# Room of 32 bytes between the parts of the activation in the feed-forward phase of a two-layer encoder

## The chip, the cores and the metric

The kernel runs on one core of a Trainium2 chip. The core has a matrix engine (PE, with its weight loads listed as PEld), a vector engine (DVE), a scalar engine (ACT), GpSimd (POOL), and a queue engine (SP) that only starts transfers here. All of them work on a memory of 128 partitions (SBUF); PE writes its sums to PSUM. The metric is the device time of one execution in microseconds (us), as the median of three runs: 2537.42 us before the change (2535.24 to 2538.15).

## The reference

The kernel computes two layers of an encoder on 512 tokens of width 1024, in float32. Each layer has a feed-forward block, a mixer of three kinds of attention, and a second feed-forward block; each sits between two RMS norms:

```python
def swiglu(x, w_gu, w_down):
    gate, up = jnp.split(x @ w_gu, 2, axis=-1)
    return (jax.nn.silu(gate) * up) @ w_down

for l in range(DEPTH):                        # DEPTH = 2, D_FF = 2816
    y = swiglu(rmsnorm(h, ffn1_pre_g[l]), ffn1_w_gu[l], ffn1_w_down[l])
    h = h + 0.5 * rmsnorm(y, ffn1_post_g[l])
    u = rmsnorm(h, mix_pre_g[l])
    ...                                       # projections, three attentions, gates
    h = h + rmsnorm(merged @ w_out[l], mix_post_g[l])
    y = swiglu(rmsnorm(h, ffn2_pre_g[l]), ffn2_w_gu[l], ffn2_w_down[l])
    h = h + 0.5 * rmsnorm(y, ffn2_post_g[l])
```

The change touches the four feed-forward blocks only.

## The kernel before

Everything is kept transposed: a tile has 128 features on the partitions and the 512 tokens along the row, which is 2048 bytes per partition. A float32 product is made of three products of the short float32 form (fp32r): each operand is split into `hi` (the value rounded) and `lo` (the rest), and `mm3` (lines 235, 236, 237) adds hi·hi, hi·lo and lo·hi in one PSUM bank. ACT writes `hi`, DVE writes `lo` by subtraction: for weights at lines 193 and 194 (tiles `wh`, `wl`, made from the raw block `wr`), for activations at lines 258 and 259 in `split`. Weights stream in by transfers that ACT's queue starts (line 179).

A feed-forward block (`ffn`) first makes 22 gate columns and 22 up columns from the normed input `X` (8 pairs `hi`, `lo`); `finish` (lines 425 to 427) scales the gate sum with `rB`, applies Silu, multiplies with the up sum and splits the result into a pair of the tag `a`. These 22 pairs, 44 tiles, are the activation's parts. Then the down projection (`end`) reads them as the moving operand: 8 output columns of 22 blocks each, the last column in two halves of the tokens, so that the norm of the first half can run beside the second. The first three columns of the next block (`begin`) also run in two halves, and two of their weight tiles are held in slots of the phase's own pool (`w`, tag `a` in a feed-forward block, `tx` in the mixer).

Memory: one pool (`sb`) lasts for the whole kernel, with X, h, the weights and the temporaries. Behind it each phase opens a pool of its own at the same place (`open_phase`), first a feed-forward pool, then a mixer pool, then a feed-forward pool, for each layer. A tile of a new phase has to wait for the last reader or writer of those tiles of the old phase that lay on the same bytes. At the start of the mixer, SP fetches from DRAM the tables `mask` (line 554) and `tab` (550) and the bias block `braw` (560), and stores h (`kept`, 544); DVE uses the masks at line 567, POOL uses `tab` at line 551.

Each engine works through its own list of instructions in order. The lists are made by a scheduler at build time, which also looks at which slots of a pool are free.

Of the kernel before, what the change touches and what calls it, by code (L numbers as in the profile page):

```python
# [10 lines left out]
F32 = mybir.dt.float32  # L11
# [5 lines left out]
P = 128  # L17
# [6 lines left out]
KF = FF // P  # L24
# [86 lines left out]
def encoder_kernel(ctx: ExitStack, tc: tile.TileContext, order, xT, wts, cols, rows, rpb, consts, tables, out):  # L111
# [12 lines left out]

    def open_phase(kind):
        pool = ExitStack()
        phase[0] = (kind, pool.enter_context(tc.tile_pool(name=nm("ph"), bufs=1, reuse_waits="tile")))
        phase[0][1].tile([P, PAD[kind]], F32, tag="pad", name=nm("pad"), bufs=1)
        return pool
    serial = [0]  # L130

    def nm(s):
        serial[0] += 1
        return f"{s}{serial[0]}"

    def big(tag, dt=F32, shape=(P, T), name="v"):
        if tag in BUFS:
            return sb.tile(list(shape), dt, tag=tag, name=nm(name), bufs=BUFS[tag])
        kind, pool = phase[0]
        return pool.tile(list(shape), dt, tag=tag, name=nm(name), bufs=ABUFS[kind][tag])  # L140

    def small(tag, w=4, bufs=4):
# [39 lines left out]
    def ensure(n):  # L182
        while stream["made"] < min(n, NTILES * 2):
            i = stream["made"]
            if i // 2 == len(stream["raw"]):
                fetch(1)
            raw = stream["raw"][i // 2][:, i % 2 * HB : i % 2 * HB + HB, :]
            if i in stream["held"]:
                tag = stream["held"][i]
                hi, lo = (big(tag, F32R, (P, HB, P), name="w") for _ in range(2))  # L190
            else:
                hi, lo = (sb.tile([P, HB, P], F32R, tag=t, name=nm(t), bufs=BUFS[t]) for t in ("wh", "wl"))
            A.activation(hi, raw, AF.Copy)  # L193
            V.tensor_tensor(out=lo, in0=raw, in1=f(hi), op=ALU.subtract)  # L194
            stream["ready"].append((hi, lo))
            stream["made"] += 1
# [12 lines left out]


    h = [big("h", name="h") for _ in range(KD)]

    def load(hs, *bs):
# [40 lines left out]
    def split(src, tag="a", scale=None, shape=(P, T)):  # L254
        hi = big(tag, F32R, shape, name="hi")
        lo = big(tag, F32R, shape, name="lo")
        if scale is None:
            A.activation(hi, src, AF.Copy)  # L258
            V.tensor_tensor(out=lo, in0=src, in1=f(hi), op=ALU.subtract)  # L259
        else:  # L260
            A.activation(hi, src, AF.Copy, scale=scale)
            V.scalar_tensor_tensor(out=lo, in0=src, scalar=scale, in1=f(hi), op0=ALU.mult, op1=ALU.subtract)
        return hi, lo
# [509 lines left out]
    for l in range(L):  # L773
        with open_phase("f"):
            refresh, X = ffn(l, 1, refresh, X)
        if l == 0:
            prepare()
        with open_phase("m"):
            refresh, X = mixer(l, refresh, X)
        with open_phase("f"):  # L780
            refresh, X = ffn(l, 2, refresh, X)
# [5 lines left out]
def build(order):  # L787
    import concourse.bacc as bacc

    nc = bacc.Bacc("TRN2", target_bir_lowering=False, num_devices=1)  # L790
    shapes = {
        "xT": (D, T),
        "wts": (NTILES, P, WB * P),
        "cols": (P, NCOLS),
        "rows": (L * ROWW,),
        "rpb": (L * 8 * 16 * RPBW,),
        "consts": (P, CONSTW),
        "tables": (P, TABLEW),
    }
    args = [nc.dram_tensor(f"in_{n}_dram", s, F32, kind="ExternalInput").ap() for n, s in shapes.items()]  # L800
    args.append(nc.dram_tensor("out_0_dram", (D, T), F32, kind="ExternalOutput").ap())
    with tile.TileContext(nc) as tc:
        encoder_kernel(tc, order, *args)
    return nc
# [35 lines left out]
```

## Time and profile before

| | |
|---|---|
| median of three runs | 2537.42 us (2535.24 to 2538.15) |
| the profiled execution's own time | 2534.24 us |
| its span, from the first to the last instruction | 2532.5 us |
| mean granted clock of the matrix engine | 0.998 of full speed |
| busy: PE, PEld, DVE, ACT, POOL | 99%, 83%, 54%, 44%, 9% of the span |

Matmuls overlap in the pipeline, and their ends are modelled: the mean duration of a 128x512 matmul is 392 ns, but the next one starts some 227 ns later. So PE's pace is read from the starts in a timeline, not from durations. "Idle before" in brackets is time in which the engine stood still ahead of a row, with the instruction that ended it.

### The profile page before, as it was taken

To read this page: it belongs to the slowest core of one execution; us is meant where nothing else is said; L and a number is where in the kernel's file an instruction comes from. 1 tells how busy PE (TensorE), PEld (TensorE's weight loads), DVE (VectorE), ACT (ScalarE), POOL (GpSimd) and SP (SyncE) were. 2 spreads that over 40 slices of the span, in tenths; PEclk is the share of its full clock that TensorE was granted. 3 is DMA by queue.
4 is the path that set the end of the run, shared out by engine and by line. 5 is a ranking of instruction groups with operands and counts; after the bars stand their busy time and mean duration, and the time that the engine had idled before them with its cause. 6 is when DMAs were issued, how large, how long until landed. Compare 5 with 4: busy or idle time off the path is not lost.

```text
span 2532.5 us, 32765 instructions
## 1 busy us (share of the span) xinstructions
PE 2506.4 (99%) x12274; PEld 2103.0 (83%) x12274; DVE 1380.1 (54%) x2687; ACT 1116.3 (44%) x2163; POOL 215.6 (9%) x197
## 2 busy tenths in 40 slices
PE   9999999999999999999999999999999999999998
PEld 8888888888778888888888888888887788888887
DVE  5444248867776464442364442488687764644423
ACT  5333245646555453333343332456465554533322
POOL 0000011001111220000110000200001112100002
PEclk9999999999999999999999999999999999999999
DMA  4232237435443322222232223374344423232222
GB/s 157 94 100 94 98 99 218 119 109 138 114 125 99 108 76 93 99 100 92 92 100 100 92 100 100 112 211 113 108 131 130 116 95 105 75 100 95 97 100 83
DMA packets 97375, 277.87 MB, mean 110 GB/s; under 512 B 13504, under 2 KB 17984, under 8 KB 97216
## 3 DMA queue, kind: packets, MB, share of 16 engines
q10 hardware_dynamic: 59616, 216.63, 25.9%
q1 hardware_dynamic: 37600, 59.15, 9.2%
q8 instruction: 96, 1.57, 0.3%
q14 instruction: 63, 0.52, 0.1%
HBM read 231.16 MB, written 6.29 MB: 94 GB/s over the span
## 4 chain that ended last, share of the span: by engine, by line
PE 91%; DVE 3%; issue 2%; DMA 1%; ACT 1%; POOL 1%; SPq 1%; POOLq 0%; DVEq 0%; ACTq 0%
PE mm L237 19%; PE mm L236 19%; PE mm L235 19%; PE at L236 9%; PE at L235 9%; PE at L237 9%; PE at L512 1%; POOL h L392 1%; PE o L515 1%; PE o L516 1%; PE at L484 1%; DMA sh<-raw 1%; PE at L269 1%; PE at L631 1%; PE at L485 1%
## 5 line engine op out<-in xcount | busy, mean ns | idle before, releaser
L193 ACT ACTIVATE wh<-wr 128x512 fp32r<-128x512 f32 x812 | 511.3, 631 | 1005.7 <-PE at L236 506.6
L194 DVE TENSOR_TENSOR wl<-wr,wh 128x512 fp32r<-128x512 f32 x812 | 582.7, 719 | 651.3 <-ACT wh L193 642.7
L237 PE MATMUL mm<-hi,wl 128*128 128x512 f32 (+1 forms) x2372 | 899.0, 379 | 4.8 <-DVE wl L194 4.4
L235 PE MATMUL mm<-hi,wh 128*128 128x512 f32 (+1 forms) x2372 | 897.1, 378 | 1.3 <-ACT wh L193 1.1
L236 PE MATMUL mm<-lo,wh 128*128 128x512 f32 (+1 forms) x2372 | 896.7, 378 | 0.1
L237 PEld LDWEIGHTS mm<-hi,wl 128*128 128x128 f32 x2372 | 447.2, 189 | 83.3 <-DVE wl L194 7.9
L235 PEld LDWEIGHTS mm<-hi,wh 128*128 128x128 f32 x2372 | 447.2, 189 | 77.8 <-ACT wh L193 1.3
L236 PEld LDWEIGHTS mm<-lo,wh 128*128 128x128 f32 x2372 | 447.3, 189 | 76.4 <-DVE lo L310 0.3
L235 PE MATMUL at<-hi,wh 128*128 128x512 f32 (+1 forms) x1028 | 394.3, 384 | 0.0
L236 PE MATMUL at<-lo,wh 128*128 128x512 f32 (+1 forms) x1028 | 393.8, 383 | 0.0
L237 PE MATMUL at<-hi,wl 128*128 128x512 f32 (+1 forms) x1028 | 393.6, 383 | 0.0
L235 PEld LDWEIGHTS at<-hi,wh 128*128 128x128 f32 x1028 | 193.5, 188 | 37.8
L237 PEld LDWEIGHTS at<-hi,wl 128*128 128x128 f32 x1028 | 193.5, 188 | 37.7
L236 PEld LDWEIGHTS at<-lo,wh 128*128 128x128 f32 x1028 | 193.4, 188 | 37.5
L304 POOL TENSOR_TENSOR ss<-ss,sq 128x512 f32<-128x512 f32 (+1 forms) x38 | 46.9, 1233 | 1391.3 <-ACT sq L303 1390.2
L427 DVE TENSOR_TENSOR t<-t,at 128x512 f32<-128x512 f32 x88 | 60.1, 687 | 127.4 <-PE at L237 124.2
L425 DVE TENSOR_TENSOR t<-mm,rB 128x512 f32<-128x512 f32 x88 | 60.5, 691 | 121.5 <-PE mm L237 121.3
L258 ACT ACTIVATE hi<-at 128x256 fp32r<-128x256 f32 (+2 forms) x168 | 75.8, 472 | 69.3 <-PE at L512 31.0
L259 DVE TENSOR_TENSOR lo<-at,hi 128x256 fp32r<-128x256 f32 (+2 forms) x168 | 87.1, 533 | 18.0 <-ACT hi L258 16.6
L392 POOL TENSOR_TENSOR h<-h,y 128x256 f32<-128x256 f32 x92 | 77.0, 867 | 83.2 <-DVE y L390 83.2
L530 POOL TENSOR_TENSOR sh<-sh,sinR 128x512 f32<-128x512 f32 x26 | 34.3, 1319 | 545.1 <-DMA sh<-raw 329.6
L497 ACT ACTIVATE s<-s,nmx 128x256 f32<-128x256 f32 (+1 forms) x128 | 70.4, 552 | 14.0 <-DVE nmx L488 7.5
(146 smaller groups left out, 2145.0 us busy)
## 6 DMA issues: line engine op xcount, KB each, us to landing
wr<-in_wts_dram ACTq DMA_DIRECT2D x413, 512.0 KB, 3.2
st<-hi SPq DMA_DIRECT2D x84, 128.0 KB, 2.3
st<-lo SPq DMA_DIRECT2D x84, 128.0 KB, 2.3
sh<-raw SPq DMA_DIRECT2D x104, 64.0 KB, 2.0
sw<-lo SPq DMA_DIRECT2D x36, 128.0 KB, 3.5
sw<-hi SPq DMA_DIRECT2D x36, 128.0 KB, 3.0
braw<-in_rpb_dram SPq DMA_DIRECT2D x16, 256.0 KB
kept<-h SPq DMA_DIRECT2D x16, 256.0 KB, 2.0
```

The costliest lines, as they stand in the source:

```text
L193: A.activation(hi, raw, AF.Copy)
L194: V.tensor_tensor(out=lo, in0=raw, in1=f(hi), op=ALU.subtract)
L235: PE.matmul(acc, w[0], x[0], start=start, stop=False)
L236: PE.matmul(acc, w[0], x[1], start=False, stop=False)
L237: PE.matmul(acc, w[1], x[0], start=False, stop=stop)
L258: A.activation(hi, src, AF.Copy)
L259: V.tensor_tensor(out=lo, in0=src, in1=f(hi), op=ALU.subtract)
L304: eng.tensor_tensor(out=self.acc[:, cs], in0=self.acc[:, cs], in1=sq[:, cs], op=ALU.add)
L392: adder.tensor_tensor(out=h[b][:, hs], in0=h[b][:, hs], in1=y[b][:, hs], op=ALU.add)
L425: V.tensor_tensor(out=t, in0=pg, in1=rB, op=ALU.mult)
L427: V.tensor_tensor(out=t, in0=t, in1=pu, op=ALU.mult)
L497: A.activation(ss[i], ss[i], AF.Exp, scale=-scale, bias=nmx[:, i : i + 1], accum_out=l[:, i : i + 1])
```

## The change

Before, the 44 parts are one tag with 44 slots, and lie against each other. Now each part gets a tag of its own (`a0` to `a43`, in the order in which the program asks for them, starting again after 44), and in the first round a small tile of 8 floats, 32 bytes, is asked for behind each.

```diff
     def open_phase(kind):
         pool = ExitStack()
+        ramp[0] = 0
...
     serial = [0]
+    ramp = [0]
...
         kind, pool = phase[0]
+        if tag == "a":
+            n = ramp[0] % (2 * KF)
+            ramp[0] += 1
+            t = pool.tile(list(shape), dt, tag=f"a{n}", name=nm(name), bufs=1)
+            if n == ramp[0] - 1:
+                pool.tile([P, 8], F32, tag=f"ap{n}", name=nm("ap"), bufs=1)
+            return t
         return pool.tile(list(shape), dt, tag=tag, name=nm(name), bufs=ABUFS[kind][tag])
```

In the program as built, the parts start at byte 135136 + 2048 n of a partition before, and at 135136 + 2080 n after (n from 0 to 43). Before, every tile of 2048 bytes in the long-lived pool and in the phases' pools starts at the same remainder modulo 2048, namely 2016; after, this still holds for all but the parts, whose starts go through all multiples of 32. The mixer's pool and the long-lived pool stay where they were. The held weights of `begin` in a feed-forward block now always lie in the first four slots.

PE's list is the same, row for row. On ACT and DVE neighbours change places at the start of each feed-forward block, and nowhere else. This is ACT's list at the start of the first block of the first layer, before: `t` are the gate sums under Silu (line 426), `hi` the parts (258), `wh` the weights (193).

```order
L193 ACTIVATE wh_521<-wr_503 128x512
L426 ACTIVATE t_537<-t_537 128x512
L258 ACTIVATE hi_455<-t_451 128x512
L193 ACTIVATE wh_548<-wr_546 128x512
L258 ACTIVATE hi_463<-t_459 128x512
L179 DMA wr_624<-in_wts_dram 128x1024
```

And after (its lines are 9 higher):

```order
L202 ACTIVATE wh_529<-wr_511 128x512
L435 ACTIVATE t_545<-t_545 128x512
L267 ACTIVATE hi_459<-t_455 128x512
L267 ACTIVATE hi_469<-t_465 128x512
L202 ACTIVATE wh_558<-wr_556 128x512
L188 DMA wr_636<-in_wts_dram 128x1024
```

The second part's `hi` has gone ahead of one weight tile (`wh_548`, now `wh_558`); DVE's `lo` and `wl` of the same tiles swap in the same way. In the other three blocks a weight tile goes ahead of one Silu, and on DVE a `lo` ahead of one line 425. This is ACT's list at the start of the second block of the first layer, before:

```order
L258 ACTIVATE hi_8815<-t_8811 128x512
L179 DMA wr_8976<-in_wts_dram 128x1024
L426 ACTIVATE t_8889<-t_8889 128x512
L193 ACTIVATE wh_8900<-wr_8898 128x512
L193 ACTIVATE wh_8916<-wr_8898 128x512
```

And after:

```order
L267 ACTIVATE hi_8865<-t_8861 128x512
L188 DMA wr_9032<-in_wts_dram 128x1024
L202 ACTIVATE wh_8954<-wr_8952 128x512
L435 ACTIVATE t_8941<-t_8941 128x512
L202 ACTIVATE wh_8970<-wr_8952 128x512
```

The Silu of the third gate column stands behind one weight tile more than before. At the entry of the mixer no list is reordered, but some waits are for other instructions, since other parts lie under the mixer's tiles. This is SP's list there with its waits, before:

```order
L554 DMA mask_3336<-in_tables_dram 128x512 [waits DMAHW2_49,DVE_49,PE_49]
L554 DMA mask_3338<-in_tables_dram 128x384 [waits DMAHW3_49,PE_49]
L560 DMA braw_3497<-in_rpb_dram 128x1x512 [waits DMAHW4_49]
L550 DMA tab_3330<-in_tables_dram 128x512 [waits DMAHW5_49,PE_49]
```

And after:

```order
L563 DMA mask_3380<-in_tables_dram 128x512 [waits DMAHW2_49,DVE_49,PE_49]
L563 DMA mask_3382<-in_tables_dram 128x384 [waits DMAHW3_49,DVE_49]
L569 DMA braw_3541<-in_rpb_dram 128x1x512 [waits DMAHW4_49]
L559 DMA tab_3374<-in_tables_dram 128x512 [waits DMAHW5_49,DVE_49]
```

The first `mask` now waits for a later matmul: for PE's count 1739 where it was 1687. `tab` waited for PE's count 1742 and now waits for a DVE instruction long before. POOL's `sinR` (line 551) now also waits for count 1742. The second layer has the same at its counts 7735, 7787 and 7790.

## Rows read from the trace of the kernel before

**Rows 1.** The page, part 1: busy time, share of the span, instructions.
```profile
span 2532.5 us, 32765 instructions
...
PE 2506.4 (99%) x12274; PEld 2103.0 (83%) x12274; DVE 1380.1 (54%) x2687; ACT 1116.3 (44%) x2163; POOL 215.6 (9%) x197
```
**Rows 2.** The page, part 4: the chain that ended last, by engine.
```profile
PE 91%; DVE 3%; issue 2%; DMA 1%; ACT 1%; POOL 1%; SPq 1%; POOLq 0%; DVEq 0%; ACTq 0%
```
**Rows 3.** Windows: stretch, length, each engine's busy us (count), granted clock, DMA.
```profile
60.00:240.00 180.00, 180.00 (x796) 149.05 (x795) 77.05 (x117) 62.90 (x100) 0.00 (x0) 1.00 0.29 97
245.00:355.00 110.00, 110.00 (x488) 91.10 (x487) 30.98 (x44) 33.16 (x55) 6.45 (x5) 1.00 0.29 96
```
**Rows 4.** PE's waits over the whole span: us in total, times, longest.
```profile
PE o L278 <- DVE ss L304: 4.7, 6, 1.4
PE mm L237 <- DVE wl L194: 4.4, 6, 1.0
...
PE at L512 <- DVE s L504: 0.2, 1, 0.2
```
**Rows 5.** Timeline of PE, gate and up columns: start us, modelled us, instruction.
```profile
99.78 0.39 PE L235 MATMUL mm<-hi,wh 128*128 128x512 f32 x1
...
105.90 0.39 PE L235 MATMUL at<-hi,wh 128*128 128x512 f32 x1
```
**Rows 6.** Timeline of PE, down projection (moving operand: the parts).
```profile
250.06 0.39 PE L235 MATMUL mm<-hi,wh 128*128 128x512 f32 x1
...
259.81 0.39 PE L236 MATMUL mm<-lo,wh 128*128 128x512 f32 x1
```
**Rows 7.** Timeline of PE, half-wide columns; the first weights are held among the parts.
```profile
15.05 0.28 PE L235 MATMUL mm<-hi,w 128*128 128x256 f32 x1
...
19.97 0.28 PE L237 MATMUL mm<-hi,wl 128*128 128x256 f32 x1
```
**Rows 8.** Timeline of PE in the mixer, four slower starts.
```profile
706.40 0.40 PE L237 MATMUL mm<-hi,wl 128*128 128x512 f32 x1
...
707.33 0.39 PE L631 MATMUL at<-st,st 128*128 128x512 f32 x1
```
**Rows 9.** Groups by form: count, busy us, mean ns.
```profile
L259 DVE TENSOR_TENSOR lo<-t,hi 128x512 fp32r<-128x512 f32 x88 | 60.9, 692 | 7.6
L425 DVE TENSOR_TENSOR t<-mm,rB 128x512 f32<-128x512 f32 x88 | 60.5, 691 | 121.5 <-PE mm L237 121.3
```
**Rows 10.** Timeline of ACT, first feed-forward block.
```profile
40.60 0.63 ACT L193 ACTIVATE wh<-wr 128x512 fp32r<-128x512 f32 x1 [0.54 <-PE at L236]
...
41.13 0.61 ACT L258 ACTIVATE hi<-t 128x512 fp32r<-128x512 f32 x1
```
**Rows 11.** Timeline of DVE, the same place.
```profile
41.26 0.69 DVE L194 TENSOR_TENSOR wl<-wr,wh 128x512 fp32r<-128x512 f32 x1
```
**Rows 12.** Timeline of PE: first matmul with that weight tile.
```profile
48.78 0.39 PE L235 MATMUL at<-hi,wh 128*128 128x512 f32 x1
```
**Rows 13.** Timeline of ACT, second block: the Silu that moves.
```profile
931.58 0.63 ACT L426 ACTIVATE t<-t 128x512 f32<-128x512 f32 x1 [1.07 <-DVE t L425]
```
**Rows 14.** Timeline of DVE: the multiplication after that Silu.
```profile
934.26 0.69 DVE L427 TENSOR_TENSOR t<-t,at 128x512 f32<-128x512 f32 x1 [0.80 <-PE at L237]
```
**Rows 15.** Timeline of SP's queue at the mixer's entry.
```profile
365.14 2.58 SPq L554 DMA_DIRECT2D mask<-in_tables_dram  x2
...
372.08 0.34 SPq L550 DMA_DIRECT2D tab<-in_tables_dram  x1
381.41 8.21 SPq L544 DMA_DIRECT2D kept<-h  x8
```
**Rows 16.** Timeline of DVE: first use of `mask` and `braw`.
```profile
387.23 0.96 DVE L567 TENSOR_TENSOR bedge<-braw,mask 128x256 f32<-128x256 f32 x1
```
**Rows 17.** Timeline of ACT: a weight block that lands late beside them.
```profile
375.59 0.63 ACT L193 ACTIVATE w<-wr 128x512 fp32r<-128x512 f32 x1 [1.25 <-DMA wr<-in_wts_dram]
```
**Rows 18.** Timeline of POOL: the rotary tables.
```profile
404.79 1.76 POOL L551 TENSOR_TENSOR sinR<-tab,rB 128x512 f32<-128x512 f32 x1
```

## The prediction

> **What bounds the kernel now.** I read the page first. PE is busy for 2506.4 of 2532.5 us [rows 1], and the chain that ended last is PE for 91% [rows 2], so time comes off only where PE's pace rises or where PE waits less. The list of PE's waits comes next: twelve entries, the first two of 4.7 and 4.4 us, the last of 0.2, all twelve together 16.1 us, 0.6% of the span [rows 4]. They lie in the mixer and at the seams between phases. Then the windows: inside a feed-forward block PE is busy for 180.00 of 180 us while the gate and up columns run, and for 110.00 of 110 us in the down projection, at granted clock 1.00 [rows 3]. No wait is left there.
>
> So the pace itself is the question, and it is read from starts. In the gate and up columns, whose moving operand X is not touched by the change, 27 steps take 105.90 - 99.78 = 6.12 us, 226.7 ns each [rows 5]. In the down projection, which reads the parts, 43 steps take 9.75 us, again 226.7 ns [rows 6]. Half-wide matmuls take 4.92 us for 41 steps, 120.0 ns each [rows 7]. At 2.4 GHz these are 544 cycles for 512 columns and 288 for 256. Each matmul pays for its columns and 32 cycles more, the same 32 at both widths.
>
> **The change, part by part.** I cost it at five places.
>
> 1. *Reads of the parts by PE.* Per block, seven of eight down columns are full: 7 x 22 x 3 = 462 matmuls of 512 columns, and the last column gives 2 x 22 x 3 = 132 of 256; with four blocks 1848 and 528, together 2376. Only their starting byte changes. The trace has one kind of start alone for all large tiles, so a new start is not shown and has to be bounded. From above: the slowest pace of a 512-column matmul that the trace keeps up is in the mixer, where four steps take 0.93 us, 232.5 ns each [rows 8], 5.8 ns over 226.7; on 2376 matmuls that is 13.8 us. From below: if the 32 extra cycles (13.3 ns) came from where the tiles start and went away, 2376 x 13.3 ns = 31.6 us. I take 0. The pace is the same to a tenth of a nanosecond for X beside a DVE that is 43% busy (77.05 of 180) and for the parts beside one that is 28% busy (30.98 of 110) [rows 3], so nothing that runs beside PE disturbs its reads, and the 32 cycles do not grow with the bytes read, as a cost of addresses would. The slower steps of rows 8 are in a stretch of the mixer with waits and other kinds of matmul, not with other starts.
>
> [...]
>
> 2. *Writes and reads of the parts by ACT and DVE.* A `lo` from two tiles with the same remainder takes 692 ns, while the multiplication at L425, with one operand in PSUM, takes 691 [rows 9]. Two SBUF operands with equal starts therefore cost 1 ns over one, and moving them apart can give back 1 ns on 88 instructions, which PE's full pace hides anyway. 0.
>
> 3. *The swap in the first block.* The weight tile's `wh` ran from 40.60 to 41.23, its `wl` from 41.26 to 41.95; PE asks for the tile at 48.78 [rows 10 to 12]. Behind a `hi` of 0.61 us and a `lo` of 0.69 us it may come 1.3 us later and is still more than 5 us early. ACT even stood idle for 0.54 us ahead of that `wh`, which the `hi` now fills. 0, and without this cover 1.3 us.
>
> 4. *The swap in the other three blocks.* The Silu, at 931.58, falls behind a weight tile of 0.63 us on ACT [rows 10] and a `lo` of 0.69 us on DVE [rows 9], so it ends at 932.2 + 1.3 = 933.5 at the latest. Its reader on DVE starts at 934.26, and what it waited for is a matmul, not the Silu [rows 13, 14]. 0; without the cover 3 x 1.3 = 3.9 us on DVE, of which PE would see little. The weight tile that goes ahead only gains.
>
> 5. *The mixer's entry.* `tab` was started at 372.08, when PE's count reached 1742 [rows 15]. The first `mask` now waits for 1739, which comes before, so it starts at most 6.9 us later than 365.14. Behind it in SP's queue stand the second `mask`, `braw` and `tab`; before, all of them went out within those 6.9 us, so now `tab` is out by 372.08 + 6.9 = 379.0 at the latest. `kept`, next in the queue, starts at 381.41 for its own reason (POOL's h) and does not move. First use of `mask` and `braw` is at 387.23 [rows 16], over 8 us after even that. POOL's `sinR` at 404.79 [rows 18] waits for a count that was reached near 372. In the other direction, a weight block landed late beside these transfers and held ACT for 1.25 us at 375.59 [rows 17]; with the tables started after it, it may come sooner. That is at most 1.25 us at each of two entries, on an engine that PE was not waiting for. I take 0 and keep -2.5 us as an end.
>
> The sum is 0: on the profiled execution 2534.24 + 0 = 2534.2 us (its span of 2532.5 and 1.7 around it). The median of the three runs is 3.2 us above that one, so the forecast for a median is **2537.4 us**. Known terms that may come out otherwise reach from -2.5 to +1.3 + 3.9 = 5.2 us.
>
> **The rivals.**
>
> *Slower: the new starts cost PE cycles.* All parts but the first of a phase now start at another remainder than the other large tiles. If this holds a read up as much as the mixer's slow steps show, the down projections lose 13.8 us, and the time is 2551 us. It decides from 2.1 ns per matmul on, where it reaches 0.2%. For it speaks only that no row has such a start; against it the even pace of rows 5 and 6. Chance 0.12. That the later tables hold DVE up at the mixer's entry belongs on the same side: it would need the transfers to take over 8 us, and costs what they take beyond it. 0.02.
>
> *Faster: equal starts are what costs the 32 cycles.* Then the down projection alone goes to 213.3 ns per matmul, and the time is 2537.4 - 31.6 = 2506 us; a part of it, if only some of the starts are freed. Against it: 32 cycles at both widths, in stages with different neighbours. Chance 0.05.
>
> *Faster at the seams.* The tables that no longer run beside the weights give up to 2.5 us, 2535 us. That is under the limit of what can be told; to count as faster, the waits at the seams would have to give twice as much. Chance of that 0.03.
>
> *The room is not there.* A tile that nobody reads or writes might be dropped. The starts in the built program are 2080 bytes apart, so I give it no chance of its own; its time would be the forecast.
>
> **How the numbers follow.** A difference of 0.2%, 5.1 us, is about what runs of this kernel can tell (the three before spread over 2.9 us). No change within that: 0.78. Slower: 0.12 + 0.02 = 0.14. Faster: 0.05 + 0.03 = 0.08. The range goes from 2530 us, the seams' gain and the spread of the runs together with a small part of the faster case, to 2547 us, which takes in the 5.2 us of the known terms and the lower two thirds of the slower rival.
>
> **What would show it.** In the changed kernel's timeline the starts in the down projection stay 226.7 ns apart; a step of 229 ns or more there, or steps that depend on which part is read, make the slower rival right, and 213 ns the faster one. The windows of the gate and up columns and of the down projections stay full. At the mixer's entry the first `mask` is started near 371 instead of 365, and `tab` behind it between 375 and 379; DVE's first line 567 (there 576) keeps its place, and PE's waits stay near 16 us. ACT's 1.25 us in front of the held weight tile shrinks. The forecast is wrong if the time moves by over 5 us, and its reason is wrong if the down projections change length while something else hides it.

## The result, and the profile after

The changed kernel takes 2543.79 us (median of 7 runs, 2543.15 to 2544.68), the kernel before 2536.69 us in 7 runs beside it (2534.83 to 2538.15). The ratio is 1.0029 [1.0017, 1.0040]: 7.1 us slower, where no change was forecast. The time lies in the predicted range (2530 to 2547 us), but on the side that was given a chance of 0.14. The profiled execution took 2543.52 us, its span is 9.2 us longer than that of before, at the same granted clock of 0.998. Page of after, part 1:

```profile
span 2541.7 us, 32772 instructions
...
PE 2514.5 (99%) x12274; PEld 2101.7 (83%) x12274; DVE 1378.9 (54%) x2687; ACT 1116.4 (44%) x2163; POOL 215.5 (8%) x197
```

Beside [rows 1], PE has the same 12274 matmuls and is busy 8.1 us longer; DVE and ACT do the same work in the same time. So the time is in PE's matmuls, and not in anything it waits for. The list of PE's waits in after (total, times, longest) confirms it; all twelve entries together are 17.0 us, where they were 16.1 [rows 4]:

```profile
PE mm L246 <- DVE wl L203: 4.9, 6, 1.0
PE o L287 <- DVE ss L313: 4.7, 6, 1.4
...
PE at L521 <- DVE s L513: 0.2, 1, 0.2
```

The windows of after (columns as in [rows 3]) show in which stage the matmuls are slower:

```profile
60.00:240.00 180.00, 180.00 (x796) 149.06 (x795) 76.86 (x116) 63.12 (x100) 0.00 (x0) 1.00 0.28 97
245.00:355.00 110.00, 110.00 (x478) 89.28 (x477) 30.55 (x43) 32.81 (x54) 6.46 (x5) 1.00 0.29 96
```

The gate and up columns have 796 matmuls in 180 us, as before. In the down projection PE is still busy for 110.00 of 110 us at granted clock 1.00, but gets through 478 matmuls where it did 488 [rows 3]. A busy share of 100% hides that; the count in brackets, or the distance of the starts, shows it. PE's timeline of after, in the gate and up columns:

```profile
99.84 0.39 PE L246 MATMUL mm<-hi,wl 128*128 128x512 f32 x1
...
105.96 0.39 PE L246 MATMUL at<-hi,wl 128*128 128x512 f32 x1
```

and in the down projection:

```profile
249.67 0.39 PE L244 MATMUL at<-hi,wh 128*128 128x512 f32 x1
...
259.86 0.40 PE L246 MATMUL at<-hi,wl 128*128 128x512 f32 x1
```

The first pair is 27 steps in 6.12 us, 226.7 ns, as in [rows 5]. The second is 44 steps in 10.19 us, 231.6 ns, where [rows 6] had 226.7. Over all four blocks the full-width steps that read parts have a mean of 231.52 ns in after and 226.67 in before. The half-wide steps of the last column (without two of some 200 ns at its seams) went the other way, from 119.9 to 117.7 ns, and those of `begin` that use weights held among the parts from 120.0 to 118.5.

The sum: 1848 x 4.85 = 8.96 us lost, 528 x 2.2 = 1.2 us and some 0.3 us in `begin` given back, together 7.5 us, against 7.1 between the medians. The profiled pair differs by 9.3 us; 0.9 of that is in the waits, and the profiled run of before, 2534.24 us, lies below all seven.

### The profile page after: what moved, and what is told of

The parts are those of the page before. It is cut to its first block, busy times and chain, and to the rows that moved or that the text cites. A ratio compares the mean times of both kernels' runs of the same rounds, so it can differ in the third digit from the quotient of the medians.

```text
span 2541.7 us, 32772 instructions
## 1 busy us (share of the span) xinstructions
PE 2514.5 (99%) x12274; PEld 2101.7 (83%) x12274; DVE 1378.9 (54%) x2687; ACT 1116.4 (44%) x2163; POOL 215.5 (8%) x197
## 4 chain that ended last, share of the span: by engine, by line
PE 72%; DVE 3%; issue 1%; ACT 1%; POOL 1%; DMA 0%; SPq 0%; POOLq 0%; DVEq 0%; ACTq 0%
PE mm L246 15%; PE mm L245 15%; PE mm L244 15%; PE at L246 7%; PE at L245 7%; PE at L244 7%; PE at L521 1%; PE at L640 1%; PE at L278 1%; DVE wl L203 1%; PE at L641 1%; PE o L525 1%; PE o L524 1%; PE at L663 0%; PE at L493 0%
```

## The experiments

What had to be told apart: do the changed neighbours and waits cost anything (the swaps), does the room as such, and if it is the starts, in relation to what? Theory A: what counts is where the moving tile starts relative to the weight tile, modulo some power of two. Theory B: relative to the part read just before. Theory C: its own start alone. In all windows below the columns are stretch, length, PE's busy us (matmuls), granted clock, DMA share, GB/s; the four stretches lie in the full-width part of the four down projections, where the kernel before has 354 or 355 matmuls in 80 us. A step is counted from the start of a matmul to the next start, and belongs to the tile that the first of the two reads. Where one time is given, it is from one execution, beside a kernel before of 2536 to 2537 us.

**The tags without the room.** The 44 tags keep the swaps and, but for a few counts at the mixer's entry (the first `mask` waits for 1737 instead of 1739, `sinR` for 1740 instead of 1742), the new waits; the parts stay against each other:

```diff
             t = pool.tile(list(shape), dt, tag=f"a{n}", name=nm(name), bufs=1)
-            if n == ramp[0] - 1:
-                pool.tile([P, 8], F32, tag=f"ap{n}", name=nm("ap"), bufs=1)
             return t
```

> The 44 tags of the change without the 32 bytes of room: the parts lie as before, but the swaps on ACT and DVE and the moved waits at the mixer's entry are those of the change. Theory 1 (the starts of the parts slow the down projection's matmuls): the full-width steps are 226.7 ns again and the time is that of before, 2537 us within 3. Theory 2 (swaps and waits are what costs): 2543 to 2545 us, with the down projection at 226.7 ns per step and the loss in PE's waits.

Measured: 2535.61 us (11 runs), ratio to before 0.9995 [0.9986, 1.0004].

```profile
260.00:340.00 80.00, 80.00 (x355) 1.00 0.29 96
1160.00:1240.00 80.00, 80.00 (x355) 1.00 0.30 99
1520.00:1600.00 80.00, 80.00 (x354) 1.00 0.28 93
2410.00:2490.00 80.00, 80.00 (x355) 1.00 0.27 93
```

The full-width steps of the down projections are back at 226.67 ns. The reordering and the waits cost nothing that these runs can tell; the loss comes with the 32 bytes.

**All parts moved together.** One tag as before, no room between parts, but the whole feed-forward pool starts 32, 64, 128 and 256 bytes further in the four blocks; then, in a second kernel, 96, 160, 192 and 224:

```diff
+    SHIFT = [32, 64, 128, 256]
-        phase[0][1].tile([P, PAD[kind]], F32, tag="pad", name=nm("pad"), bufs=1)
+        extra = SHIFT.pop(0) // 4 if kind == "f" else 0
+        phase[0][1].tile([P, PAD[kind] + extra], F32, tag="pad", name=nm("pad"), bufs=1)
```

> One tag as before, no room between the parts; the whole pool of a feed-forward phase starts later, by 32, 64, 128 and 256 bytes in the four blocks. All parts of a block share one start modulo 256, which differs from that of the weights and of X. Theory A (a part's start against the start of the weight tile that is loaded beside it): the down projections of the first three blocks leave 226.7 ns per full-width step, by some 2 to 9 ns up, or down; the fourth stays if the pattern repeats every 256 bytes. Theory B (a part's start against that of the part read before and after): all four stay at 226.7 ns, and the time is that of before.

Measured: 2543.75 us.

```profile
260.00:340.00 80.00, 80.00 (x345) 1.00 0.28 93
1160.00:1240.00 80.00, 80.00 (x351) 1.00 0.29 99
1520.00:1600.00 80.00, 80.00 (x345) 1.00 0.28 92
2410.00:2490.00 80.00, 80.00 (x355) 1.00 0.30 99
```

The steps are 233.34 ns at 32 bytes, about 229 at 64, 233.32 at 128 and 226.67 at 256. There is no room between the parts here, and every part has the same remainder as its neighbours, so B alone cannot be the cause. A distance of 256 bytes is as good as none. Nor is it ACT and DVE writing at the same time: they are busy for some 30% and 28% of the first block's down projection (32.61 and 30.43 of 110 us, where before had 33.16 and 30.98 [rows 3]), and not one of its 461 steps is under 230 ns, where all 461 of before take 226 or 227.

> The same with 96, 160, 192 and 224 bytes. Theory A: other paces than 226.7 ns in the down projections, one for each shift; the half-wide steps of the last column, 120.0 ns before and 117.8 ns with the room, move too. Theory B: 226.7 and 120.0 ns in all four.

Measured: 2545.09 us.

```profile
260.00:340.00 80.00, 80.00 (x345) 1.00 0.28 93
1160.00:1240.00 80.00, 80.00 (x343) 1.00 0.28 92
1520.00:1600.00 80.00, 80.00 (x344) 1.00 0.27 92
2410.00:2490.00 80.00, 80.00 (x345) 1.00 0.28 98
```

233.37 ns at 96, about 234.3 at 160, 233.33 at 192 and 233.3 at 224. Of the eight remainders modulo 256 in steps of 32 only the weights' own is at 226.7. The half-wide steps of the last column do the opposite. In the order 32, 64, ..., 256 they take 116.8, 115.9, 120.0, 118.7, 117.9, 115.3, 118.3 and 119.9 ns. PE's timeline at 192 bytes, in the third block's last column:

```profile
1624.04 0.28 PE L237 MATMUL mm<-hi,wh 128*128 128x256 f32 x1
...
1629.93 0.28 PE L238 MATMUL mm<-lo,wh 128*128 128x256 f32 x1
```

That is 52 steps in 5.89 us, 113.3 ns, against 120.0 in [rows 7]. The full-width step at 192 bytes takes 6.7 ns more than with equal starts (233.33 against 226.67 ns), the half-wide one in this stretch 6.7 ns less: the same amount, once up and once down. The two are not equal in general: at 96 bytes the full-width step is 233.4 ns and the half-wide one stays at 120.0.

**Weights moved instead of parts.** `wh` and `wl` start 32 bytes further in the whole kernel. X stays; the parts move along in blocks 1 and 2 and stay in 3 and 4:

```diff
+    BACK = [0, 8, 0, 8, 8, 8]
-        phase[0][1].tile([P, PAD[kind]], F32, tag="pad", name=nm("pad"), bufs=1)
+        back = BACK.pop(0)
+        phase[0][1].tile([P, PAD[kind] - back], F32, tag="pad", name=nm("pad"), bufs=1)
...
+                if i == 0:
+                    sb.tile([P, 8], F32, tag="wroom", name=nm("wroom"), bufs=1)
```

> The weight tiles wh and wl start 32 bytes later in every phase, X stays. The parts start 32 bytes later too in the first two feed-forward blocks, and stay in the last two; no room between them. Theory A (a part's start against the weights' start, modulo 256): the down projections are at 226.7 ns per full-width step in blocks 1 and 2, where both moved, though the same move of the parts alone gave 233.3; in blocks 3 and 4, where only the weights moved, some 233 ns (a difference of 224, which gave 232.8); the gate and up columns, X against the moved weights, go from 226.7 to some 233 ns in all four blocks, and the whole to 2575 to 2595 us. Theory C (the part's own start alone, whatever the weights' is): blocks 1 and 2 near 233 ns, blocks 3 and 4 and all gate and up columns at 226.7, 2540 us.

Measured: 2577.49 us. The first window is that of the gate and up columns, which read the unmoved X:

```profile
60.00:240.00 180.00, 180.00 (x773) 1.00 0.28 94
...
260.00:340.00 80.00, 80.00 (x355) 1.00 0.29 96
1160.00:1240.00 80.00, 80.00 (x354) 1.00 0.30 98
1520.00:1600.00 80.00, 80.00 (x345) 1.00 0.27 90
2410.00:2490.00 80.00, 80.00 (x344) 1.00 0.28 92
```

This separates A from C. The parts of blocks 1 and 2 are moved and run at 226.7 ns, as the weights moved with them; the parts of blocks 3 and 4 are unmoved and run at 233.3, the pace that 224 bytes had before (not the 232.8 of the expectation). These two down projections begin only at 1533 and 2439 us here, so the last two windows hold gate and up columns as well, which are as slow. X has not moved by a byte, and its steps go from 226.7 to 233.3 ns in all four blocks (773 matmuls in 180 us instead of 796). What counts is the difference between the two starts: 226.7 ns with both moved, 233.3 with one of them moved. It also shows what an equal start is worth where the weights are off against X in the whole kernel and against half of the parts: 41 us, 1.6%.

**Which parts, and how fine.** Four layouts, one per block: 256 bytes behind every third part; all `hi` together and all `lo` 32 bytes further; the same with 128 bytes; 64 bytes behind every part.

```diff
+    LAYOUT = [
+        [(n, 256 * (n % 3 == 2)) for n in range(N)],
+        [(n, 32 * (n == N - 2)) for n in hilo],
+        [(n, 128 * (n == N - 2)) for n in hilo],
+        [(n, 64) for n in range(N)],
+    ]
```

> A layout of its own in each block. Block 1: 256 bytes of room behind every third part, so that starts differ, but never modulo 256. Block 2: all hi parts together and all lo parts behind them, 32 bytes further on, so that only the change between hi and lo is a change of start, and hi has the weights' remainder. Block 3: the same with 128 bytes. Block 4: 64 bytes of room between each two parts. If the pattern repeats every 256 bytes, block 1 has 226.7 ns per full-width step, else some 231. Theory A: in blocks 2 and 3 the steps that read hi stay near 226.7 ns and those that read lo are longer. Theory B: in blocks 2 and 3 the steps at a change between hi and lo are longer, and a hi that follows a hi is not. Block 4: near 231 ns by both, if 64 bytes are enough to tell starts apart.

Measured: 2542.68 us; in the four stretches 355, 347, 351 and 347 matmuls. 256 bytes cost nothing (226.67 ns). With `lo` 128 bytes off, the steps that read `lo` take 234.2 ns and those that read `hi` 226.2: only the displaced tile pays. With `lo` 32 bytes off, though, the steps that read the equally placed `hi` take 231.0 ns as well as `lo`'s 233.0. So a step can also pay for its neighbour's start, and a mixed layout does not cost the mean of its tiles' costs (here 231.7 ns instead of 228.9). With 64 bytes behind every part the mean is 232.1 ns, and the parts with the weights' own remainder, at 233.5, are the slowest. The change is such a mixed layout: its parts take all eight remainders modulo 256, and the 336 steps that read one with the weights' remainder take 231.9 ns, hardly less or more than the rest. Theory A holds for layouts with one distance throughout; it does not give the single step of a mixed one, where the neighbours' starts count too, so B is not wholly wrong there.

The second kernel of this kind moves 16 of the 44 parts by 4, 8, 16 and 240 bytes in the four blocks:

```diff
+            if 4 <= n < 20:
+                t = pool.tile([P, T + 64], dt, tag=f"a{n}", name=nm(name), bufs=1)
+                return t[:, fine[0] : fine[0] + T]
```

> The parts are where they were modulo 256, but for 16 of the 44 (the first eight pairs), which start 4, 8, 16 and 240 bytes further on, one value for each of the four blocks. Theory A with a pattern in steps of 32 bytes or more: 4, 8 and 16 bytes leave 226.7 ns per full-width step, and 240 is like 224, near 233 ns. Theory A with a finer pattern: other paces at 4 to 16 bytes already, by a few ns, perhaps below 226.7.

Measured: 2541.94 us. Steps that read the displaced parts take 236.6, 233.6, 231.6 and 233.3 ns, the others 226.7 to 227.1. Even 4 bytes cost 10 ns, the most of all distances; no distance gave a mean full-width step under 226.7. PE's timeline of the first 48 steps at 4 bytes, 11.35 us:

```profile
251.45 0.40 PE L251 MATMUL mm<-hi,wh 128*128 128x512 f32 x1
...
262.80 0.39 PE L251 MATMUL mm<-hi,wh 128*128 128x512 f32 x1
```

The half-wide steps that read displaced parts take 122.6, 120.0, 118.9 and 117.3 ns here, so the smallest distance slows them too.

**The change with 256 bytes.** If A is all, room is harmless as soon as it is a multiple of 256 bytes. To keep the pool small, it stands behind every third part alone:

```diff
+    LAYOUT = [[(n, 256 * (n % 3 == 2)) for n in range(N)] for _ in range(4)]
```

> The change with another room: tags of their own as in the change, but 256 bytes behind every third part, so that no start changes modulo 256. Theory A: 226.7 ns per full-width step in all four down projections and the time of before, 2537 us within 3. If room as such cost something, 2540 us or more.

Measured: 2535.88 us (11 runs), ratio 1.0000 [0.9991, 1.0009].

```profile
260.00:340.00 80.00, 80.00 (x355) 1.00 0.29 95
1160.00:1240.00 80.00, 80.00 (x355) 1.00 0.30 99
1520.00:1600.00 80.00, 80.00 (x355) 1.00 0.30 99
2410.00:2490.00 80.00, 80.00 (x355) 1.00 0.30 99
```

Tags, room and moved parts are all there, and the loss is gone. In the program as built, every engine's list and every wait is that of the change, so nothing but the places of the parts differs between the two.

**Is anything left to gain?** All large tiles already share one remainder. The one wide moving operand that doesn't is the identity matrix, 96 bytes off: it serves 520 transposes of 128 columns, and 80 matmuls of line 269, which are no transposes and of which the profile lists two records each. Two kernels give it the large tiles' remainder, or one 64 bytes behind it:

```diff
-PAD = {"f": 168, "m": 168}
+PAD = {"f": 104, "m": 104}
...
+    cp.tile([P, 40], F32, tag="croom", name="croom")
```

> The kernel before, with the identity matrix (the moving operand of some 700 transposes of 128 columns, lines 269, 465, 512, 654) brought to the same remainder modulo 256 bytes as the large tiles: 160 bytes of room behind the constants, everything behind them 160 bytes further, the phases' pools at a start with that same remainder. Before, the identity starts 96 bytes short of that remainder. Theory A (unequal remainders of moving operand and weights cost time) in its plain form: if a transpose loses 4 to 5 ns as a full-width step does, 700 of them give back up to 3 us: 2533 to 2536 us. If narrow steps behave as the half-wide ones, which ran 1 to 4.6 ns faster with unequal starts, it is 0 to 3 us slower: 2537 to 2540 us. Everything else stays at 226.7 ns. A difference of 3 us is at the edge of what the runs can tell, so the pace of the transposes in the trace decides.

> The same with 96 bytes of room: the identity then starts 64 bytes behind the large tiles' remainder modulo 256 bytes, where the half-wide steps were among their fastest (115.9 ns against 119.9). If narrow steps follow the half-wide ones, the transposes run 1 to 4 ns shorter than with equal starts (e8_align_cons) and the time is 0.7 to 3 us below that kernel's; if they follow the full-width ones, 2 to 5 ns longer, and 1.4 to 3.5 us above it.

Measured: 2536.4 and 2535.59 us (11 runs each), both with the ratio 0.9999 [0.9990, 1.0008]. Groups by form, first before and then with equal starts (columns as in [rows 9]):

```profile
L512 PE MATMUL at<-cons,s 128*128 128x128 f32 x320 | 49.7, 276 | 0.2 <-DVE s L504 0.2
```

```profile
L513 PE MATMUL at<-cons,s 128*128 128x128 f32 x320 | 49.7, 276 | 0.0
```

Those transposes start 109 ns apart (median) in all three kernels. They are plain float32 and not fp32r, and narrower; whether either of the two exempts them was not tried. The expectations, 1 to 5 ns per transpose in one direction or the other, missed, and no version beats the kernel before by more than the runs' spread. These kernels moved everything behind the constants, parts, X and weights alike, by 160 and by 96 bytes, and the full-width steps stayed at 226.7 ns: at these two distances the tiles' own remainder made no difference, as A says.

## Why the prediction was wrong, by its own steps

**The failed step is the first: "I take 0" for the reads of the parts.** The rival "the new starts cost PE cycles" was right. It priced all 2376 matmuls at 5.8 ns, 13.8 us; measured were +4.85 ns on the 1848 full-width ones and -2.2 ns on the 528 half-wide ones, 7.8 us in all and a good half of the rival's price. The mean over all of them, 3.3 ns, lies above its point of decision of 2.1 ns. That the price was of the right size is luck: in the program as built the matmuls of [rows 8], from which it was taken, have equal starts themselves.

What led to 0 was a reading of [rows 5] and [rows 6] that they could not carry. The pace was even to a tenth of a nanosecond because X, parts and weights all had one remainder: with the parts alone moved by 32 bytes it was 233.34 ns, with parts and weights moved 226.7. Rows with one value of a quantity are no evidence for other values, however even they are; the text said that no row showed another start and then counted the even pace against the rival. That nothing running beside PE disturbs it agrees with the traces as far as they go: in before every full-width step of the four down projections takes 226 or 227 ns, beside a DVE that is busy for 28% of the first one's stretch [rows 3]. It was beside the point: what counts is how the starts of PE's own operands stand to each other. The weights moved alone cost X's unmoved steps 6.6 ns each, so a step depends on where both kinds of tile start.

The second argument, that 32 extra cycles at both widths cannot come from addresses, fell as well. Its cycles are an estimate from [rows 5] and [rows 7]: 256 columns more take 226.7 - 120.0 = 106.7 ns, which is 2.4 columns per ns, and at one column per cycle 13.3 ns, 32 cycles, are left over at either width. Two widths always leave one common rest; the 384-column steps of line 485 in before come near it, with a median of 175 ns over 64 steps where this line gives 173.3. But with parts 192 bytes off the rest is no longer common: 20.0 ns for the full-width step (233.3 ns) and 6.7 for the half-wide one (113.3 ns in the stretch shown). Some of this time does come from where tiles start; of the starts run, the equal one gives 13.3 ns at both widths. The other side, that full-width steps would speed up to 213 ns, did not occur at any of the distances run: the lowest mean of a down projection was 226.67.

**Step 2 held.** In after the `lo` from two tiles with unequal starts takes 691 ns, where it was 692 [rows 9]:

```profile
L268 DVE TENSOR_TENSOR lo<-t,hi 128x512 fp32r<-128x512 f32 x88 | 60.5, 691 | 7.6
L434 DVE TENSOR_TENSOR t<-mm,rB 128x512 f32<-128x512 f32 x88 | 60.4, 690 | 121.5 <-PE mm L246 121.4
```

**Steps 3 and 4 held**, as the kernel with tags alone shows as a whole. Single rows agree: DVE's list of after in the first block has

```profile
40.79 1.28 DVE L268 TENSOR_TENSOR lo<-t,hi 128x512 fp32r<-128x512 f32 x2
42.00 0.68 DVE L203 TENSOR_TENSOR wl<-wr,wh 128x512 fp32r<-128x512 f32 x1
```

The delayed `wl` starts 0.74 us later than in [rows 11], and PE asks for that tile at 49.07, 6.4 us after it is done.

**Step 5 held.** SP's queue of after at the mixer's entry:

```profile
374.00 0.86 SPq L563 DMA_DIRECT2D mask<-in_tables_dram  x2
374.90 0.77 SPq L569 DMA_DIRECT2D braw<-in_rpb_dram  x1
375.78 0.35 SPq L559 DMA_DIRECT2D tab<-in_tables_dram  x1
383.77 7.99 SPq L553 DMA_DIRECT2D kept<-h  x8
```

`kept` and everything that hangs on h come 2.4 us later than in [rows 15]: 2.0 us is the first block's loss, and 0.3 us was there before its down projection. Less that, the first `mask` is at 371.6 and `tab` at 373.4, as expected or earlier. DVE's first use keeps its place behind `kept`, and ACT's wait of 1.25 us in front of the held weight tile is gone:

```profile
389.57 0.96 DVE L576 TENSOR_TENSOR bedge<-braw,mask 128x256 f32<-128x256 f32 x1
```

```profile
376.52 0.62 ACT L202 ACTIVATE w<-wr 128x512 fp32r<-128x512 f32 x1
```

With these 2.4 us the `w` would have started at 375.59 + 2.4 = 378.0; it started at 376.52, so it comes 1.5 us sooner. PE gained nothing by it, as its waits show, 17.0 us against 16.1: the end of -2.5 us that was kept in the range was not there.

## What to carry to other kernels

Where PE is busy all the time, read its pace from the starts and its matmul count per window, since the busy share cannot show a slower step (110.00 of 110 us with 488 matmuls and with 478); and ask of every layout edit whether it changes where the moving tile starts relative to the weight tile. Here an equal remainder modulo 256 bytes is worth 1 to 4% of a full-width fp32r step (226.7 ns against 229 to 236.6), so room between tiles was free in multiples of 256 bytes and cost at every other distance that was run. When a trace holds only one value of what a change varies, take the bound from the other side seriously: a steady row is no evidence for a value that it does not contain.

## What the runs showed of the hardware that was not expected

- Where one distance holds over a stretch of steps, a 512-column fp32r step takes 226.7 ns when moving tile and weight tile start at the same remainder modulo 256 bytes, and 229 to 237 ns otherwise (4 bytes 236.6, 8 bytes 233.6, 16 bytes 231.6, 32 bytes 233.3, 64 bytes about 229, 96 to 240 bytes 233.3 to 234.3).
- A 256-column step takes 119.9 ns with equal starts, 120.0 at 8 and at 96 bytes, 122.6 at 4 bytes, and less at all other distances run (115.3 to 118.9).
- It is the difference that counts: a step of unmoved tiles against weights moved 32 bytes takes 233.3 ns, as with parts moved alone, and moving both together is free (226.7).
- In a mixed layout a tile with the weights' remainder is slow too (231.9 ns in the change, 233.5 with 64 bytes behind every part).
- Open: what in a step takes the time; why the sign mostly turns with the width; how much of a step's cost comes from its neighbour's start; why steps differ where all parts are equally far off (at 64 bytes a step from `lo` to `hi` takes 226.0 ns, one from `hi` to `lo` 231.7); and whether the weight tile that counts is the step's own or the next one, whose load is listed within 4 ns of the step's start for some 98% of the full-width steps in before and after. The weight tiles of the full-width steps all had one remainder in each run, so no run can tell the two apart.
